# A planner's step table, landing time and ranks replaced, and one input load moved to ScalarE's queue, in a hybrid encoder layer

## The chip, the cores and the metric

The kernel runs on one core of a Trainium2 chip. The metric is the device time of one execution in microseconds (us). Five engines work beside each other: TensorE (PE, with its weight loads as PEld), VectorE (DVE), ScalarE (ACT), GpSimd (POOL) and SyncE (SP); SP issues most of the transfers.

## The reference

One encoder layer on two sequences of 512 tokens (prompt and sample), width 1024, all in float32:

```python
def rms_norm(x, g):
    xf = x.astype(jnp.float32)
    y = xf * lax.rsqrt(jnp.mean(xf * xf, axis=-1, keepdims=True) + EPS)
    return (y * g.astype(jnp.float32)).astype(x.dtype)

def swiglu(x, w_gate, w_up, w_down):
    return (jax.nn.silu(x @ w_gate) * (x @ w_up)) @ w_down
```

The layer is a half-weighted SwiGLU FFN (inner width 2816), a mixing block, a second such FFN and a final norm. The mixing block normalizes once and projects once; from that come grouped-query attention (8 query heads, 2 key heads of 64, rotary angles, softmax over 512 keys) and a bidirectional mLSTM memory (4 heads of 128, exponentials of gate sums as weights on q k^T, a row norm). Each is projected to the model width, both are gated per channel by a sigmoid and merged, and one output projection follows.

## The kernel before

Precision is kept by splitting: a float32 value becomes a high part (ScalarE copies it to fp32r) and a low part (VectorE subtracts the high part), and each product is three matmuls (high x high, high x low, low x high) of 512 columns. The FFNs and the gate projections use seven products of half blocks in place of eight, with sums of blocks of weights and inputs written by VectorE. So a weight costs a load on SP, a "high" on ScalarE (L247, L832, L2111) and a "low" on VectorE (L248, L835, L2114) before TensorE may use it, and a product costs an evacuation of its bank.

The first FFN fills 0 to about 640 us, the mixing block of both sequences about 640 to 1440, the second FFN the rest. The FFNs' order is written by hand. The order of the mixing block, with its seams to the FFNs, comes from a planner that runs while the kernel is built (`class Plan`, L719). Each piece of work is a task with an engine, a step (how long the engine is held), an end (when its result may be used), its dependencies, and the slots it needs and frees (banks, buffers). The planner keeps a clock per engine; at each step it takes, over all engines, the task that can start first, and among those of one engine that can start within 0.01 us the one with the lowest rank. The rank is

```python
t.rank = pri + self.n * 1e-3 + RANK.get(f"{self.part} {eng} {fn.__name__}", 0)
```

with a priority by kind (0 urgent, 2 and 3 weights, 5 for long rows of filling matmuls), the number of the task, and an entry of `RANK` (L702) for the part of the block, the engine and the function. The steps come from `ACT_STEP` and `DVE_STEP` (L789) by the width of the instruction; a helper's `more` adds to one, and `n` multiplies one for chains of small instructions. A transfer is given its bytes at 400 KB per us and `LANDING` (L791) us. None of this runs on the chip: the emitted order is pinned, each engine works through its own list in that order, and semaphores make it wait where an input is not there.

Names that the change and the steps below touch, with their lines before the change:

- `sums_stage` (L2163): scales the rows by their norm (L2167 on ScalarE, L2168 on VectorE), transposes them on TensorE (L1702), copies them out with the gain (L2197, tiles `t`), stores part of them to `xn1buf` (L2205), and builds sums and differences of blocks (L2217 on VectorE, high L2209 on ScalarE, low L2212 on VectorE, tiles `xc`). `seven` (matmuls at L2125) uses them for the gates, L2155 evacuates its banks `mm` to tiles `f`, and L2289 to L2302 make sums of weight blocks.
- `gates_rest` (L2268): the products that need these sums; L2316 takes their bank `pss`.
- kv, k, q and gates of the mixing block: L883 matmuls in token blocks, kv high and low at L816 and L819; the gate sums' matmuls L1055 need `Lt` (L1061).
- attention: scores L1225, after transposes of q at L1149 copied out at L1152.
- the memory heads, four for each sequence: 20 exponentials of 128 columns for each head (L1430, tiles `t` from `box` and `st`), q k^T products (L1441, bank `pss`), transposes of the weighted product (L1500), copied out (L1504) and split (L1508), output products with `Vm` (L1515, bank `pso`), squares of the output (L1526), their transposes (L1535). L853 are matmuls of the projections for the next head.
- the merge of the memory (`up_mem`): L1586 multiplies a gate onto the product in a bank `mm` and so frees the bank, L1589 adds it to `mg`, L816 and L819 make the high part `mh` and the low part `ml`; the output projection (L883, with `mh` and `ml`) follows. Beside it the next sequence's rows are transposed (L1702), copied out (L2090), stored to `xnbuf` (L2096) and split (L2097, L2098).
- `load_x` (L1708): loads chunks of the transposed input; L1761 and L1762 split them for the first products.

## Time and profile before

| | |
|---|---|
| time, median of 3 runs | 2045.89 us (2043.71 to 2048.75) |
| the profiled execution's own time | 2045.49 us |
| its span, first to last instruction | 2043.7 us |
| mean granted TensorE clock | 0.998 |
| TensorE busy, share of the span | 2024.0 us, 99% |
| TensorE weight loads busy | 1675.0 us, 82% |
| VectorE busy | 1593.8 us, 78% |
| ScalarE busy | 969.0 us, 47% |
| first matmul starts, last one ends | 1.04 us, 2033.3 us |

A row of the timeline reads: start in us from the span's start, length in us, engine, line of the kernel, operation, output and inputs by tile name, shapes, how many in a row, and in brackets how long the engine stood idle before it and what ended that. "SPq" and "ACTq" are the issues of transfers by SP and ScalarE. A row of waits reads: engine, operation's tile and line, the releaser, total us, times, longest. Lines are those of the kernel before; from L718 on the changed kernel has the same code one line further down.

### The profile page before, as it was taken

How to read it: one execution, taken by the hardware profiler on the slowest of the kernel's cores; microseconds unless marked ns; L12 is line 12 of the kernel's file. 1: busy time of each engine (PE TensorE's matmuls, PEld its weight loads, DVE VectorE, ACT ScalarE, POOL GpSimd, SP SyncE). 2: the span in 40 equal slices, each digit the busy share in tenths (PEclk: the TensorE clock that was granted, in tenths of full speed). 3: DMA queues.
4: the chain of work that ended last, by engine and by line, in shares of the span. 5: the costliest groups of instructions: out<-in, count | busy, mean ns of one | idle time of the engine just before them, and what ended most of it. 6: DMA issues, size and time to landing. Idle time of an engine off the chain costs nothing.

```text
span 2043.7 us, 26087 instructions
## 1 busy us (share of the span) xinstructions
PE 2024.0 (99%) x9340; PEld 1675.0 (82%) x9340; DVE 1593.8 (78%) x2532; ACT 969.0 (47%) x1620; POOL 24.5 (1%) x49
## 2 busy tenths in 40 slices
PE   9999999999999999999999999999999999999997
PEld 7888888888888788887888888888788888888886
DVE  7997888786796764896887866875888787776687
ACT  7543434342227533676644774655443444343224
POOL 0000000001000000000000000000000000000001
PEclk9999999999999999999999999999999999999999
DMA  9556555799774645312344322464464644389753
GB/s 340 185 169 223 182 189 202 245 367 354 249 253 148 218 141 181 107 45 83 124 132 163 130 83 73 149 220 148 133 236 164 218 166 153 134 296 398 271 199 143
DMA packets 149633, 389.02 MB, mean 190 GB/s; under 512 B 15232, under 2 KB 15296, under 8 KB 147712
## 3 DMA queue, kind: packets, MB, share of 16 engines
q1 hardware_dynamic: 148784, 385.60, 54.6%
q0 software_dynamic: 432, 1.25, 0.2%
q8 instruction: 73, 1.20, 0.2%
q10 hardware_dynamic: 288, 0.52, 0.1%
q14 instruction: 56, 0.46, 0.1%
HBM read 269.31 MB, written 118.00 MB: 190 GB/s over the span
## 4 chain that ended last, share of the span: by engine, by line
PE 89%; DVE 4%; ACT 3%; DMA 2%; issue 1%; SPq 0%; DVEq 0%; ACTq 0%
PE pss L292 17%; PE pst L292 11%; PE mm L853 10%; PE mm L292 8%; PE mm L553 7%; PE mm L883 7%; PE pst L553 4%; PE pss L553 4%; PE pss L2125 3%; PE pso L553 2%; PE pso L883 2%; PE pst L2125 2%; PE mm L2125 2%; PE pss L1225 1%; PE pst L1249 1%
## 5 line engine op out<-in xcount | busy, mean ns | idle before, releaser
L292 PE MATMUL pss<-xc,w 128*128 128x512 f32 x1632 | 389.7, 389 | 2.5 <-DVE t L322 0.9
L292 PEld LDWEIGHTS pss<-xc,w 128*128 128x128 f32 x1632 | 305.9, 188 | 68.2 <-DVE t L322 1.7
L247 ACT ACTIVATE w<-wr 128x1024 fp32r<-128x1024 f32 (+2 forms) x123 | 127.5, 1038 | 223.2 <-PE pst L292 118.0
L248 DVE TENSOR_TENSOR w<-wr,w 128x1024 fp32r<-128x1024 f32 (+2 forms) x123 | 147.0, 1197 | 60.2 <-ACT w L247 60.0
L292 PE MATMUL mm<-xc,w 128*128 128x512 f32 x792 | 190.4, 390 | 0.8 <-ACT xc L1761 0.6
L553 PE MATMUL mm<-w,rt 128*128 128x512 f32 x792 | 185.3, 389 | 0.0
L292 PEld LDWEIGHTS mm<-xc,w 128*128 128x128 f32 x792 | 148.3, 188 | 32.5 <-ACT xc L1761 1.3
L553 PEld LDWEIGHTS mm<-w,rt 128*128 128x128 f32 x792 | 148.5, 188 | 30.8
L292 PE MATMUL pst<-xc,w 128*128 128x512 f32 x528 | 127.0, 389 | 0.0
L292 PE MATMUL pst<-xc,f 128*128 128x512 f32 x528 | 126.8, 389 | 0.0
L835 DVE TENSOR_TENSOR w<-wr,w 128x1024 fp32r<-128x1024 f32 (+1 forms) x80 | 93.7, 1171 | 30.1 <-ACT w L832 29.3
L292 PEld LDWEIGHTS pst<-xc,w 128*128 128x128 f32 x528 | 99.1, 188 | 20.7
L292 PEld LDWEIGHTS pst<-xc,f 128*128 128x128 f32 x528 | 99.1, 188 | 20.6
L613 ACT ACTIVATE w<-t 128x512 fp32r<-128x512 f32 x82 | 51.6, 632 | 122.1 <-PE pst L553 63.6
L613 ACT ACTIVATE w<-wr 128x512 fp32r<-128x512 f32 x72 | 44.7, 631 | 128.2 <-PE pso L553 67.7
L832 ACT ACTIVATE w<-wr 128x1024 fp32r<-128x1024 f32 (+1 forms) x80 | 80.8, 1015 | 43.4 <-PE pso L883 26.8
L553 PE MATMUL pss<-w,rt 128*128 128x512 f32 x396 | 94.4, 389 | 0.5 <-ACT w L613 0.5
L553 PE MATMUL pst<-w,rt 128*128 128x512 f32 x396 | 94.0, 389 | 0.0
L553 PEld LDWEIGHTS pss<-w,rt 128*128 128x128 f32 x396 | 74.3, 188 | 16.2 <-ACT w L613 0.9
L553 PEld LDWEIGHTS pst<-w,rt 128*128 128x128 f32 x396 | 74.3, 188 | 15.4
L2125 PE MATMUL mm<-xc,w 128*128 128x512 f32 x360 | 83.9, 391 | 1.3 <-ACT f L2155 1.3
L2125 PEld LDWEIGHTS mm<-xc,w 128*128 128x128 f32 x360 | 67.1, 188 | 15.6 <-ACT f L2155 1.8
(404 smaller groups left out, 3896.3 us busy)
## 6 DMA issues: line engine op xcount, KB each, us to landing
rt<-rbuf SPq DMA_DIRECT2D x154, 512.0 KB, 5.7
rbuf<-t SPq DMA_DIRECT2D x72, 512.0 KB, 3.5
wr<-in_ffn_w_gate_dram SPq DMA_DIRECT2D x60, 512.0 KB, 4.3
wr<-in_w_in_cols_dram SPq DMA_DIRECT2D x48, 512.0 KB, 4.0
wr<-in_ffn_w_up_dram SPq DMA_DIRECT2D x44, 512.0 KB, 3.7
rbuf<-f SPq DMA_DIRECT2D x30, 512.0 KB, 4.0
rbuf<-tab SPq DMA_DIRECT2D x30, 512.0 KB, 3.9
wr<-in_ffn_w_down_dram SPq DMA_DIRECT2D x48, 256.0 KB, 6.3
```

The costliest lines, as they stand in the source:

```text
L247: pin(nc.scalar.activation(t[:, 0], src, AF.Copy))
L248: pin(V_.tensor_tensor(t[:, 1], src, f(t[:, 0]), op=ALU.subtract))
L292: pin(nc.tensor.matmul(p, a[:, k, :], xt[:, b, k, :], start=(first and k == 0 and i == 0), stop=(k == HK_ - 1 and i == 2), skip_group_chec ...
L553: nc.tensor.matmul(p, r[:, b, d * P:(d + 1) * P], u[:, a, :], start=(first and q == 0 and k == 0), stop=(q == len(us) - 1 and k == 2), ski ...
L613: nc.scalar.activation(hi, src, AF.Copy)
L832: own(nc.scalar.activation(c["hi"], c["raw"], AF.Copy))
L835: own(V_.tensor_tensor(c["lo"], c["raw"], f(c["hi"]), op=ALU.subtract))
L853: own(nc.tensor.matmul(b["p"], w_[:, k, cols], x_, start=(k == 0 and i == 0), stop=(k == n - 1 and i == 2)))
L883: own(nc.tensor.matmul(b[q][:, :N], x_[:, q * P:(q + 1) * P], w_[:, kl, :], start=(k == 0 and i == 0), stop=(k == KD - 1 and i == 2)))
L1225: own(nc.tensor.matmul(p, G["qT"][:, h, b * P:(b + 1) * P], G["kv"][:, h // 4 * 2 + j, :], start=(j == 0), stop=(j == 1)))
L1249: own(nc.tensor.transpose(p[:, b * P:(b + 1) * P], G["e", h, b // 2][:, b % 2, kb * P:(kb + 1) * P], ident))
L2125: own(nc.tensor.matmul(bank[name], left()[a][:, k, :], xcl[m][:, y, k, :], start=bool(first) and k == 0 and i == 0, stop=(k == HK_ - 1 and ...
```

## The change

Four things are replaced. `RANK` gets other keys and values (61 entries before, 65 now, few in common). The step tables and `LANDING` get other numbers, and so do eight `n` and `more` arguments. Where the planner's tasks are the same, their order is not: of the rows in which the emitted lists are compared (repeats folded), 3439 lines differ on TensorE, 2096 on ScalarE, 3124 on VectorE, 885 on SP, all between the first FFN's end and the second one's beginning but for one: the load of the second input chunk goes from SP, behind the first half weight and the gain, to ScalarE's queue, behind the first chunk and ahead of the table load. The numbers of instructions of each engine stay as they were, but for that transfer.

```diff
-    RANK = {"gsums ACT copy": 10.5, "k0 DVE k_scale": 10, "keys0 PE turn_k": 4, "rotate0 ACT high": -0.5,
...
-            "up_mem1 PE fn": -0.79, "up_mem1 DVE add": 7, "after1 PE turn": 1.17, "next ACT left_a": -5.5}
+    RANK = {"gsums ACT <lambda>": 5, "gsums ACT copy": 5, "grest ACT p_high": -7, "kv0 ACT raw": 0.09,
...
+            "sums ACT high": 2, "sums DVE low": 8}

-    ACT_STEP = {8: 0.2, 32: 0.2, 128: 0.3, 256: 0.33, 384: 0.45, 512: 0.51, 544: 0.7, 1024: 0.97}
-    DVE_STEP = {8: 0.11, 32: 0.12, 64: 0.14, 96: 0.28, 128: 0.26, 256: 0.34, 384: 0.48, 512: 0.61, 544: 0.65, 1024: 1.14}
-    SPARE, LANDING = 0.12, 1.9
+    ACT_STEP = {8: 0.12, 32: 0.15, 128: 0.18, 256: 0.33, 384: 0.48, 512: 0.59, 544: 0.6, 1024: 1.03}
+    DVE_STEP = {8: 0.11, 32: 0.12, 64: 0.14, 96: 0.28, 128: 0.26, 256: 0.34, 384: 0.5, 512: 0.67, 544: 0.7, 1024: 1.16}
+    SPARE, LANDING = 0.12, 2.3

-        root_q = dve(32, hold("rq", lambda: rstd_cols(G["ssq"], 32, DA, own)), reds, 0, n=18)
+        root_q = dve(32, hold("rq", lambda: rstd_cols(G["ssq"], 32, DA, own)), reds, 0, n=19.5)
-        t = act(32, gate_exp, [t], 0, more=2.8)
+        t = act(32, gate_exp, [t], 0, more=1.55)
...
-        scaled = dve(32, scales, [u], 1, (), ["pt"], n=20)
+        scaled = dve(32, scales, [u], 1, (), ["pt"], n=21.3)
...
     load_x(0, 0, 1, nc.scalar)
+    load_x(0, 1, 2, nc.scalar)
     load_half(0, 0)
     pin(nc.sync.dma_start(g1, I["ffn1_norm"]))
     warm = cpool.tile([P, 1], F32, name="warm")
     nc.scalar.activation(warm, ones[:, 0:1], AF.Silu)
-    load_x(0, 1, 2)
     load_x(0, 2, 3)
```

The lines left out are further entries of `RANK` and five more such arguments: the attention's `exp` (`more` 0.2 to 0.12), two `sq` (0.2 to 0.04) and two `left_sums` (`n` 5 to 4.25 and to 5.6).

**First place: ScalarE's list in the gate sums, about 670 to 685 us.** `w_` are weights made high, `f2_354` takes evacuated banks `mm_`, `xc_364` and `xc_367` are the first two block sums of the second half; `t2_356` is what one VectorE instruction writes only after the store from it has landed. Before:

```order
L2111 ACTIVATE w_386_5037<-wr_374_4907 128x1024
L2197 ACTIVATE t2_357_4830<-pst_377_4921,gain_2_93 128x512
L2197 ACTIVATE t2_357_4830<-pst_380_4939,gain_2_93 128x512
L2155 ACTIVATE f2_354_4827<-mm_385_5017 128x512
L2209 ACTIVATE xc_364_4864<-t2_357_4830 128x1024
L2209 ACTIVATE xc_367_4867<-t2_356_4829 128x1024
L2155 ACTIVATE f2_354_4827<-mm_383_4980 128x512
L2111 ACTIVATE w_388_5081<-wr_378_4927 128x1024
L2155 ACTIVATE f2_354_4827<-mm_387_5061 128x512
L2209 ACTIVATE xc_365_4865<-t2_316_4679 128x1024
```

and now:

```order
L2112 ACTIVATE w_386_5034<-wr_370_4889 128x1024
L2156 ACTIVATE f2_354_4827<-mm_385_5016 128x512
L2198 ACTIVATE t2_356_4829<-pss_377_4924,gain_2_93 128x512
L2198 ACTIVATE t2_357_4830<-pst_378_4931,gain_2_93 128x512
L2198 ACTIVATE t2_356_4829<-pss_379_4939,gain_2_93 128x512
L2198 ACTIVATE t2_357_4830<-pst_380_4947,gain_2_93 128x512
L2210 ACTIVATE xc_364_4864<-t2_357_4830 128x1024
L2156 ACTIVATE f2_354_4827<-mm_383_4979 128x512
L2112 ACTIVATE w_388_5078<-wr_372_4899 128x1024
L2156 ACTIVATE f2_354_4827<-mm_387_5055 128x512
L2210 ACTIVATE xc_367_4867<-t2_356_4829 128x1024
```

Before, `xc_367`, which waits for VectorE and the store, stands ahead of the evacuation of `mm_383` and all that follows; now the evacuations of `mm_383` and `mm_387` stand ahead of it, and the four copies with the gain stand behind the evacuation of `mm_385`.

**Second place: ScalarE's list in the first memory head of the first sequence, about 960 to 970 us.** `Vm_733` is the value tile's last high part, `t2_749` to `t2_763` take the exponentials, `pst_747` and `pst_748` hold the third and the fourth transposed block, `pso_` the head's output. Before:

```order
L816 ACTIVATE Vm_733_7326<-pso_740_7382 128x512
L1430 ACTIVATE t2_749_7513<-box_468_5958,st_513_6301 128x128
L1430 ACTIVATE t2_750_7516<-box_468_5958,st_513_6301 128x128
L1430 ACTIVATE t2_749_7513<-box_468_5958,st_513_6301 128x128 x4
L1430 ACTIVATE t2_750_7516<-box_468_5958,st_513_6301 128x128 x2
L1504 ACTIVATE t2_759_7547<-pst_747_7494 128x512
L1430 ACTIVATE t2_750_7516<-box_468_5958,st_513_6301 128x128 x2
L1504 ACTIVATE t2_761_7558<-pst_748_7507 128x512
L1430 ACTIVATE t2_762_7564<-box_468_5958,st_513_6301 128x128
L1430 ACTIVATE t2_763_7567<-box_468_5958,st_513_6301 128x128
L832 ACTIVATE w_764_7569<-wr_752_7524 128x1024
```

and now, from the third exponential on (the last copy of `Vm` and two exponentials stand ahead):

```order
L1431 ACTIVATE t2_750_7515<-box_468_5958,st_511_6292 128x128
L1431 ACTIVATE t2_751_7518<-box_468_5958,st_511_6292 128x128
L1431 ACTIVATE t2_749_7513<-box_468_5958,st_511_6292 128x128 x4
L1431 ACTIVATE t2_750_7515<-box_468_5958,st_511_6292 128x128 x4
L1431 ACTIVATE t2_751_7518<-box_468_5958,st_511_6292 128x128 x4
L1505 ACTIVATE t2_762_7563<-pst_747_7494 128x512
L1431 ACTIVATE t2_763_7568<-box_468_5958,st_511_6292 128x128 x3
L1505 ACTIVATE t2_765_7578<-pst_748_7507 128x512
L1431 ACTIVATE t2_763_7568<-box_468_5958,st_511_6292 128x128 x2
L833 ACTIVATE w_766_7587<-wr_754_7532 128x1024
L833 ACTIVATE w_767_7596<-wr_756_7538 128x1024
L1527 ACTIVATE t2_768_7599<-pso_757_7542 128x512
```

Before, 8 exponentials stand between the last copy of `Vm` and the copy of `pst_747`; now 15 stand there, 3 more ahead of the copy of `pst_748`, and two weights in a row ahead of the squares.

**Third place: VectorE's list at the end of the second sequence's merge, about 1352 to 1360 us.** `mm_1389` (before) and `mm_1380` (now) are the last banks of the merge, freed by the gate; `ml_` are low parts that wait for ScalarE's high parts. Before:

```order
L835 TENSOR_TENSOR w_1379_11213<-wr_1362_11111,w_1379_11213 128x1024
L819 TENSOR_TENSOR ml_1375_11181<-mg_1034_9329,mh_1374_11180 128x512 x2
L2098 TENSOR_TENSOR xc_1292_10726<-f2_1383_11230,xc_1292_10726 128x512
L1586 SCALAR_TENSOR_TENSOR t2_1340_10997<-t2_1340_10997,mm_1382_11223 128x512
L2098 TENSOR_TENSOR xc_1292_10726<-f2_1383_11230,xc_1292_10726 128x512
L2098 TENSOR_TENSOR xc_1292_10726<-f2_1387_11256,xc_1292_10726 128x512
L1589 TENSOR_TENSOR mg_1034_9329<-mg_1034_9329,t2_1338_10988 128x512
L2098 TENSOR_TENSOR xc_1292_10726<-f2_1387_11256,xc_1292_10726 128x512
L1589 TENSOR_TENSOR mg_1034_9329<-mg_1034_9329,t2_1338_10988 128x512
L1589 TENSOR_TENSOR mg_1034_9329<-mg_1034_9329,t2_1339_10992 128x512
L819 TENSOR_TENSOR ml_1375_11181<-mg_1034_9329,mh_1374_11180 128x512 x3
L1586 SCALAR_TENSOR_TENSOR t2_1340_10997<-t2_1340_10997,mm_1389_11272 128x512
```

and now:

```order
L820 TENSOR_TENSOR ml_1376_11200<-mg_1029_9313,mh_1375_11199 128x512 x3
L1587 SCALAR_TENSOR_TENSOR t2_1340_11003<-t2_1340_11003,mm_1374_11185 128x512
L1587 SCALAR_TENSOR_TENSOR t2_1341_11009<-t2_1341_11009,mm_1377_11207 128x512
L836 TENSOR_TENSOR w_1373_11181<-wr_1361_11124,w_1373_11181 128x1024
L1587 SCALAR_TENSOR_TENSOR t2_1341_11009<-t2_1341_11009,mm_1380_11230 128x512
L836 TENSOR_TENSOR w_1379_11222<-wr_1362_11129,w_1379_11222 128x1024
L836 TENSOR_TENSOR w_1382_11251<-wr_1364_11133,w_1382_11251 128x1024
L1590 TENSOR_TENSOR mg_1029_9313<-mg_1029_9313,t2_1339_11000 128x512
L1590 TENSOR_TENSOR mg_1029_9313<-mg_1029_9313,t2_1340_11003 128x512
L2099 TENSOR_TENSOR xc_1290_10718<-f2_1386_11267,xc_1290_10718 128x512
L820 TENSOR_TENSOR ml_1376_11200<-mg_1029_9313,mh_1375_11199 128x512
```

Before, the last gate stands behind three low parts `ml_1375`; now the last gate stands ahead of the additions and the splits of the transposed rows.

More of the change, by code (lines that the diff above doesn't have):

```diff
@@ L700, in encoder @@
     outs_of = []
[L702 removed]
[3 rows of a table removed]
[L706 to L712 removed]
[3 rows of a table removed]
[L716 to L717 removed]
+    RANK = {"gsums ACT <lambda>": 5, "gsums ACT copy": 5, "grest ACT p_high": -7, "kv0 ACT raw": 0.09,
+            "k0 DVE k_cos": 14.5, "q0 SP w_fetch": -7.19, "gates0 DVE <lambda>": 3, "keys0 PE turn_k": 51.5,
+            "rotate0 DVE low": -2, "mem_qk0 SP w_fetch": -2, "mem_qk0 DVE w_low": 15, "mem_qk0 ACT high": -24.5,
[4 rows of a table added]
+            "up_mem0 DVE add": 6, "after0 DVE low": 4.5, "kv1 ACT w_high": -1.5, "kv1 DVE w_low": 5.5,
+            "kv1 ACT raw": 0.5, "q1 ACT w_high": -1.5, "out1 ACT w_high": -1.5, "out1 DVE w_low": -14,
[6 rows of a table added]
+            "up_mem1 PE fn": -4.5, "up_mem1 DVE add": 7.5, "after1 ACT copy": -3, "sums ACT copy": 30.5,
+            "sums ACT high": 2, "sums DVE low": 8}
     class Plan:
@@ L1241, in mix @@
                 first = [exps[h - h % 2, 0]] if h % 2 or b else []
-                exps[h, b] = act(512, exp, [u, *first] + ([exps[h, b - 1]] if b % 2 else []), 1, ["prob"] if b % 2 == 0 else (), ["ps"], more=0.2)
+                exps[h, b] = act(512, exp, [u, *first] + ([exps[h, b - 1]] if b % 2 else []), 1, ["prob"] if b % 2 == 0 else (), ["ps"], more=0.12)
             bank = ("o", "mm")[h % 2]
@@ L1622, in done @@
                     u = dve(512, add, [t, into[h]], 1)
-                    ends.append(act(512, sq, [u], 1, (), [bank_of(q)], more=0.2))
+                    ends.append(act(512, sq, [u], 1, (), [bank_of(q)], more=0.04))
                     dma(lambda: nc.sync.dma_start(x2buf[1][:, h, q, :], x()), [u], 2, kb=256)
```

14 lines of the change are left out of this document (3 added, 11 removed), and 16 rows, old and new, of the table RANK.

## The prediction

> **What bounds the kernel now.** I read the page first: the span and the chain that ended last.
>
> ```profile
> span 2043.7 us, 26087 instructions
> ...
> PE 89%; DVE 4%; ACT 3%; DMA 2%; issue 1%; SPq 0%; DVEq 0%; ACTq 0%
> ```
>
> TensorE holds 89% of the last chain. Then the table by windows, for the stretch from 640 to 1440 us in which the planner writes the order; its columns are the length, the busy time of TensorE, of its weight loads, of VectorE, ScalarE and GpSimd (number of instructions), the granted clock, the DMA share and GB/s.
>
> ```profile
> 640.00:1440.00 800.00, 795.36 (x3918) 660.10 (x3917) 598.10 (x1131) 471.86 (x905) 2.70 (x20) 1.00 0.41 135
> ```
>
> TensorE is busy 795.36 of 800 us there, at full clock. The change adds no matmul and removes none, so it can only move the time in which TensorE waits: 4.6 us here, two stalls at the seam behind it (0.57 and 0.69, below) and one of 0.44 at the start. Two rows of TensorE's waits that no later part shows (total us, times, longest):
>
> ```profile
> PE pss L1702 <- ACT xs L2167: 0.4, 1, 0.4
> ...
> PE pst L1055 <- DVE Lt L1061: 0.2, 1, 0.2
> ```
>
> A stall costs a little more than the idle time that is recorded. In the timeline of TensorE (start, length, line, operation, count, idle time before it with its releaser):
>
> ```profile
> 962.16 0.96 PE L1515 MATMUL pso<-t,Vm 128*128 128x512 f32 x3 [0.28 <-DVE Vm L819]
> ...
> 967.39 0.61 PE L853 MATMUL mm<-xc,w 128*128 128x512 f32 x2
> 968.58 0.66 PE L1535 MATMUL pst<-ident,t 128*128 128x128 f32 x4 [0.58 <-ACT t L1526]
> ...
> 1399.10 8.10 PE L2125 MATMUL mm<-xc,w 128*128 128x512 f32 x35
> ...
> 1433.69 6.74 PE L2125 MATMUL mm<-xc,w 128*128 128x512 f32 x29
> ```
>
> 35 matmuls of the last two kinds take 8.10 us and 29 take 6.74, so one more takes 0.227. Two start at 967.39, the next was due at 967.84 and came at 968.58: 0.74 us late for 0.58 us recorded. With 0.16 us for each of some eleven stalls the planned part with its seam can give back 4.6 + 1.3 + 1.8 = 7.7 us and the start 0.6. **All of it is 8 us, 0.4% of the time**; on the other side there is no such floor.
>
> The sum is made against the profiled execution, 2045.49 us (2043.7 us of span and 1.8 us around it). The median of the runs shown is 2045.89, so 0.4 us is added at the end. A measurement of this kernel can tell about 0.3%, 6.1 us, from no change.
>
> **The start.** The second input chunk is issued by ScalarE behind the first instead of by SP behind the first weights and the gain.
>
> ```profile
> 1.63 1.38 SPq L1709 DMA_DIRECT2D xt<-in_x_prompt_t_dram  x3
> ```
>
> ```profile
> 0.72 0.41 ACTq L1709 DMA_DIRECT2D xt<-in_x_prompt_t_dram  x1
> ...
> 7.11 2.01 ACT L1761 ACTIVATE xc<-xt,g 128x512 fp32r<-128x512 f32 x3 [0.83 <-DMA xt<-in_x_prompt_t_dram]
> ```
>
> ```profile
> 7.88 0.50 PE L292 MATMUL mm<-xc,w 128*128 128x512 f32 x1 [0.44 <-ACT xc L1761]
> ```
>
> SP issued three chunks in 1.38 us, 0.46 us each; ScalarE's own first issue ends at 0.72 + 0.41 = 1.13, so the chunk leaves at about 1.14 instead of 1.63, and the two behind it on SP move up by 0.46. ScalarE waited 0.83 us for the second chunk and TensorE then 0.44 us. I take **-0.4 us**. Bounds: the whole stall, -0.6, and 0 if the landing is set by the traffic and not by the issue. What is queued behind the new issue on ScalarE is its table load and the warm-up activation; they slide by 0.4 us, and the time in which ScalarE waits for the first weights covers them. Without that cover the start would lose those 0.4 us again.
>
> **First transposes and the gate sums, 642 to 693 us.** In the new order the first transposes stand 13 matmuls (13 x 0.227 = 2.9 us) later, behind the scaling that they waited for, but the second half of that scaling also stands later on ScalarE, behind two weight copies. Of the 0.6 us (0.4 recorded + 0.16) I take **-0.3**, between -0.6 and +0.3.
>
> ScalarE, VectorE and TensorE from the timeline, and the store from the table of transfers (count, size, median us from issue to landing):
>
> ```profile
> 671.66 0.63 ACT L2155 ACTIVATE f<-mm 128x512 f32<-128x512 f32 x1
> 672.13 1.10 ACT L2209 ACTIVATE xc<-t 128x1024 fp32r<-128x1024 f32 x1
> 677.17 1.06 ACT L2209 ACTIVATE xc<-t 128x1024 fp32r<-128x1024 f32 x1 [3.94 <-DVE t L2217]
> 678.14 0.58 ACT L2155 ACTIVATE f<-mm 128x512 f32<-128x512 f32 x1
> ```
>
> ```profile
> 675.91 1.23 DVE L2217 TENSOR_TENSOR t<-t,t 128x1024 f32<-128x1024 f32 x1 [2.63 <-DMA xn1buf<-t]
> ...
> 692.30 1.23 DVE L2114 TENSOR_TENSOR w<-wr,w 128x1024 fp32r<-128x1024 f32 x1 [3.16 <-ACT w L2111]
> ...
> 698.75 3.49 DVE L2114 TENSOR_TENSOR w<-wr,w 128x1024 fp32r<-128x1024 f32 x3
> ```
>
> ```profile
> 678.77 14.58 PE L2125 MATMUL mm<-xc,w 128*128 128x512 f32 x63 [1.34 <-ACT f L2155]
> ...
> 700.03 3.03 PE L2125 MATMUL pss<-xc,w 128*128 128x512 f32 x12 [0.34 <-DVE w L2114]
> ```
>
> ```profile
> xn1buf<-t SPq DMA_DIRECT2D x2, 512.0 KB, 6.1
> ```
>
> The row at 678.77 is the longest stall. VectorE waits 2.63 us for a store to land, ScalarE's L2209 (677.17) waits for VectorE, and the evacuation L2155 that TensorE needs (678.14) stands behind L2209. In the new order (first place in the section on the change) that evacuation, a weight copy and another evacuation stand ahead of the L2210 that depends on the store. So 1.34 + 0.16 go: **-1.5** (bounds -1.5 and 0). The price is that the four copies that feed the stores now all stand behind the evacuation that ran at 671.66, so the stores leave near 674.5 (four copies of 0.6 us from 672.1); before, all four stood ahead of it. With the 6.1 us of the last row they land between 680 and 681, where VectorE went on at 675.91 before. It has one weight copy and one subtraction less to do behind that point (2 x 1.13 us, from the three in 3.49), and so ends its chain about 4.6 - 2.3 = 2.3 us later; it had 3.16 us of idle time ahead of 692.30, so I take **0**, up to +1.0 if both stores are slow. **Behind that**, the low half of the second weight of the gates stood behind six instructions on VectorE (it is the first of the three at 698.75) and now follows the first low half directly: **-0.5** for 0.34 + 0.16; 0 if another wait takes its place.
>
> [...]
>
> **Lt and the other small ones.** The tiny matmuls that wait for Lt (L1055) stand later than Lt's new place on VectorE needs: **-0.3**. The wait at L883 for the low half of kv stays, since the weight copy that holds VectorE up there still stands ahead. The first attention scores now stand four matmuls (0.9 us) behind the last transposes of q, and two copies of 0.6 us stand between: **+0.3**, bounds 0 and +0.5.
>
> **The first part of the memory heads, 940 to 1020 us.** Here I expect a loss.
>
> ```profile
> 961.28 2.44 ACT L1430 ACTIVATE t<-box,st 128x128 f32<-128x128 f32 x8
> 963.62 0.59 ACT L1504 ACTIVATE t<-pst 128x512 fp32r<-128x512 f32 x1
> ```
>
> ```profile
> L1430 ACT ACTIVATE t<-box,st 128x128 f32<-128x128 f32 x160 | 49.7, 393 | 0.1
> ```
>
> Eight exponentials took 2.34 us (961.28 to 963.62), 0.293 each from start to start; the 393 ns of the last row overlap. The planner had 0.30 us for a 128-wide ScalarE step and now has 0.18. The new order (second place) puts 15 of them, not 8, between the last copy of Vm and the copy L1505 that TensorE's third output product needs: 15 x 0.293 = 4.4 us, where the new table sees 2.7. On the clock of before: exponentials 961.28 to 965.7, copy 965.7 to 966.3; TensorE begins the first output product at 962.16 as before, when the low half of Vm is there, has 12 matmuls ahead of the third (2.7 us) and reaches it at 964.9: it waits 1.4 us. Three more exponentials and the next copy end at 967.6 (0.6 us more of waiting), then two exponentials and the weight copy at 969.2 (0.7 more), then another weight copy and L1527 at 970.6, which the squares wait for. The squares ran at 968.58 before, so this place loses 970.6 - 968.6 = **+2.0**. At the next two heads 13 exponentials stand ahead of L1527: 13 x (0.293 - 0.18) = 1.5 us more than the planner thinks, of which I take **+0.8** and **+0.5**, because memory projections stand beside them as cover. Bounds for the three: 0 (the projections cover all) and +6 (2.0 at each). For the heads of the second sequence I take nothing: there the exponentials stand ahead of waits that are late anyway.
>
> **Out projection, 1357 us.**
>
> ```profile
> 1357.60 0.73 PE L883 MATMUL mm<-w,mh 128*128 128x512 f32 x2 [0.94 <-DVE t L1586]
> ```
>
> ScalarE's copy L2090 waited for a store, three low parts L819 on VectorE waited for what stands behind it on ScalarE, and the gate L1586 that frees TensorE's bank stood behind them. In the new order (third place) all gates of that part stand ahead of the low parts and the transposes come after the last unit: **-1.1** (bounds -1.1 and 0).
>
> **The seam to the second FFN, 1440 to 1450 us.**
>
> ```profile
> 1441.45 2.58 PE L292 MATMUL pss<-xc,w 128*128 128x512 f32 x10 [0.57 <-DVE w L2114]
> ...
> 1448.12 2.14 PE L292 MATMUL pss<-xc,w 128*128 128x512 f32 x8 [0.69 <-DVE t L322]
> ```
>
> Two stalls: 0.57 us on the low half of a weight, and 0.69 on L322. The first goes, since that weight is written four instructions earlier on VectorE. For the second the answer is open: a subtraction on a late-loaded weight (L268, which followed L322 before) now stands ahead of the work that leads to L322, but TensorE also has ten more matmuls (2.3 us) ahead of its wait for L322. If that load takes the 6.1 us of the store above, the seam loses up to 1.2 us net; if it takes 4 us, it gains 1.1. I take **0**.
>
> **Sum:** -0.4 - 0.3 - 1.5 - 0.5 - 0.3 + 0.3 + 2.0 + 0.8 + 0.5 - 1.1 = -0.5. 2045.49 - 0.5 + 0.4 = **2045.4 us**: what the new order takes out at the two long stalls it gives back at the memory heads. With every bound on its good side the terms make -0.6 - 0.6 - 1.5 - 0.5 - 0.3 - 1.1 - 1.1 = -5.7, so 2040.2; with every one on its bad side 0.3 + 1.0 + 0.5 + 6 + 1.2 = +9.0, so 2054.9.
>
> **Rivals.** *The stalls go and nothing comes back*: projections stand beside the exponentials as cover. For it: between these heads TensorE has units of 24 matmuls, 5.4 us each. Against it: the waiting copy stands in ScalarE's own queue behind the exponentials, so cover on TensorE must stand ahead of the waiting matmul, and at the first head there is none. -4.1 in all: 2041.8; with the seam's gain 2040.7.
>
> *Slower, through the step of 0.18 us*: my reading of the five other heads is too kind, and each pays what the first does. It decides where 11 or more exponentials stand between the last thing released and a copy that TensorE waits for (11 x 0.113 = 1.2 us of error, more than the 0.9 us of four matmuls). With 2.0 us at each of 7 further heads instead of 1.3 for two: +12.7, so 2058.1; with half of that 2051.8. For it: 160 exponentials x 0.113 = 18 us that the new planner does not see. Against it: ScalarE is busy 472 of the 800 us, so most copies find it idle.
>
> *The change doesn't do what it says*: TensorE is never short of ready matmuls for long, so another order moves nothing that can be seen: 2045.9.
>
> **How the numbers follow.** Forecast (2042.5 to 2049.5) 0.45; nothing moves 0.15, inside the same band; stalls gone 0.17; slower through the exponentials 0.23. Faster by over 0.3% (below 2039.8) needs the second rival and more than I can find: 0.12. Slower by over 0.3% (above 2052) is most of the third and some of the forecast's bad side: 0.25. Within 0.3%: 0.63. The range takes in the good bounds and half of the slower rival: 2040 to 2053.
>
> **What would show it.** Right: no TensorE wait on the evacuation of line 2156 near 678 us, none on L1587 near 1357, and new waits of some 1.4 us on the output product L1516 and of 0.5 to 1 on L1536 near 962 to 971, with 15 exponentials in a row on ScalarE just before them, 0.293 us apart. Wrong: if these exponentials stand under running matmuls (then the second rival), or if waits on L1516 and L1536 come at all eight heads, or if a store that takes over 7 us stalls the gates at 693.

## The result, and the profile after

The changed kernel takes 2050.88 us (median; 2047.64 to 2054.59), the kernel before 2045.64 us in the same series (2043.71 to 2049.22). The ratio is 1.0022, with a 95% interval of 1.0016 to 1.0029: **4.5 us slower** by the ratio, which is not the quotient of the two medians (they differ by 5.2 us). The forecast was 2045.4 us; the time lies inside its range of 2040 to 2053, and inside the 0.3% that it called "same", but outside the likeliest case (2042.5 to 2049.5), and the forecast had the time fall a little where it rose. The profiled execution took 2049.88 us, 4.4 more than the one of before.

The page of the changed kernel, its span and the shares of the last chain by engine:

```profile
span 2048.0 us, 26069 instructions
...
PE 85%; DVE 3%; ACT 2%; DMA 2%; issue 1%; SPq 0%; DVEq 0%; ACTq 0%
```

The bound is the same, TensorE; its busy time is 2024.9 us against 2024.0. So the 4.3 us of span are time in which it waits or runs slowly, and the table by windows says in which stretch. Of before (columns as in the prediction; the second number is TensorE's busy time):

```profile
640.00:800.00 160.00, 157.77 (x711) 128.49 (x710) 107.65 (x141) 74.98 (x110) 0.00 (x0) 1.00 0.51 172
900.00:1100.00 200.00, 199.13 (x1015) 166.12 (x1014) 156.65 (x349) 123.41 (x258) 1.36 (x10) 1.00 0.33 107
...
1440.00:1500.00 60.00, 58.74 (x258) 47.93 (x258) 47.92 (x62) 22.77 (x31) 0.00 (x0) 1.00 0.54 176
```

and of after:

```profile
640.00:800.00 160.00, 159.97 (x725) 131.41 (x724) 109.20 (x142) 76.73 (x112) 0.00 (x0) 1.00 0.52 178
900.00:1100.00 200.00, 195.72 (x989) 161.95 (x988) 151.47 (x343) 121.72 (x254) 1.35 (x10) 1.00 0.32 103
...
1440.00:1500.00 60.00, 56.70 (x242) 46.12 (x241) 47.68 (x61) 22.93 (x31) 0.00 (x0) 0.97 0.48 157
```

In the first row TensorE is now hardly ever idle: 2.2 us won. In the second, the memory heads, it idles 4.3 us in place of 0.9. In the last, the seam to the second FFN, it idles 3.3 in place of 1.3, and the granted clock is 0.97, where before has 1.00. TensorE's waits of after name both places (total us, times, longest):

```profile
PE pst L292 <- ACT t L326: 3.2, 1, 3.2
PE pst L1536 <- ACT t L1527: 2.9, 4, 0.9
```

**The seam.** TensorE's timeline of after around it:

```profile
1446.71 1.52 PE L292 MATMUL mm<-xc,w 128*128 128x512 f32 x6
1451.47 3.35 PE L292 MATMUL pst<-xc,w 128*128 128x512 f32 x7 [3.24 <-ACT t L326]
```

ScalarE's timeline of after there:

```profile
1449.88 1.06 ACT L247 ACTIVATE w<-wr 128x1024 fp32r<-128x1024 f32 x1 [6.26 <-DVE wr L271]
1450.84 0.58 ACT L326 ACTIVATE t<-pst 128x512 f32<-128x512 f32 x1
```

and VectorE's:

```profile
1446.47 0.69 DVE L270 TENSOR_TENSOR wr<-tab,wr 128x512 f32<-128x512 f32 x1
1448.55 0.69 DVE L268 TENSOR_TENSOR t<-wr 128x512 f32<-128x512 f32 x1 [1.39 <-DMA wr<-in_ffn_w_up_dram]
1449.16 0.68 DVE L271 TENSOR_TENSOR wr<-wr 128x512 f32<-128x512 f32 x1
```

Read upward from TensorE: it wants the bank `pst` again, which L326 evacuates. L326 takes half a microsecond and TensorE had gone on from that bank by 1446.7, but on ScalarE it stands behind the weight copy L247, L247 needs VectorE's L271, and L271 stands behind L268, the first of four sums of halves (one addition, three subtractions) for the *next* pair of weights, whose load lands at 1448.5. In the kernel before, L268 stood behind L271, L248 and L322. VectorE's timeline of before:

```profile
1443.70 0.69 DVE L270 TENSOR_TENSOR wr<-tab,wr 128x512 f32<-128x512 f32 x1
1444.43 0.69 DVE L271 TENSOR_TENSOR wr<-wr 128x512 f32<-128x512 f32 x1
1446.25 1.23 DVE L248 TENSOR_TENSOR w<-wr,w 128x1024 fp32r<-128x1024 f32 x1 [1.13 <-ACT w L247]
1447.39 0.68 DVE L322 TENSOR_TENSOR t<-t,pss 128x512 f32<-128x512 f32 x1
1448.61 0.69 DVE L268 TENSOR_TENSOR t<-wr 128x512 f32<-128x512 f32 x1 [0.54 <-DMA wr<-in_ffn_w_up_dram]
```

Two more things differ. VectorE comes to L270 2.8 us later than before (1446.47 against 1443.70), and TensorE's second product into `pst` stands ahead of the one into `pss`, where before it stood behind it. And the seven matmuls behind the wait take 3.35 us, twice their usual time; the windows there show why (the granted clock is the third number from the end):

```profile
1451.40:1454.00 2.60, 2.53 (x6) 2.05 (x7) 2.60 (x4) 0.54 (x2) 0.00 (x0) 0.50 0.21 60
1454.00:1457.00 3.00, 3.00 (x13) 2.39 (x13) 0.10 (x1) 0.00 (x0) 0.00 (x0) 0.87 0.31 123
```

0.50 for 2.6 us and 0.87 for 3 us make 2.6 + 3 x 0.13/0.50 = 3.4 us at half the clock, which costs 1.7 us in this execution.

**The first memory head.** ScalarE's timeline of after:

```profile
958.00 0.60 ACT L817 ACTIVATE Vm<-pso 128x512 fp32r<-128x512 f32 x1 [1.23 <-PE pso L884]
958.49 4.48 ACT L1431 ACTIVATE t<-box,st 128x128 f32<-128x128 f32 x15
962.88 0.58 ACT L1505 ACTIVATE t<-pst 128x512 fp32r<-128x512 f32 x1
...
967.20 0.58 ACT L1527 ACTIVATE t<-pso 128x512 f32<-128x512 f32 x1
```

VectorE's, one row:

```profile
960.67 0.69 DVE L1451 SCALAR_TENSOR_TENSOR t<-pss,t 128x512 f32<-128x512 f32 x1 [1.15 <-ACT t L1431]
```

and TensorE's:

```profile
961.42 0.96 PE L1442 MATMUL pss<-qk 128*128 128x512 f32 x3 [0.95 <-DVE t L1451]
...
966.40 0.73 PE L854 MATMUL mm<-xc,w 128*128 128x512 f32 x2 [0.31 <-ACT w L833]
967.83 0.65 PE L1536 MATMUL pst<-ident,t 128*128 128x128 f32 x4 [0.70 <-ACT t L1527]
```

The 15 exponentials take 962.88 - 958.49 = 4.39 us, 0.293 each, as forecast, where the planner counts 0.18. TensorE feels them first at the q k^T product L1442, which wants a bank that VectorE's L1451 frees, and L1451 waits for exponentials (0.95 us); then at the weight of L854 (0.31) and at the squares (0.70).

For the experiments one number for each stretch is needed that clock and waits both enter: **lost time**, the time from start to start of successive matmuls beyond the step that their kind takes when nothing waits (0.2267 us for 512 columns, 0.124 for 272, 0.109 for 128), summed over the stretch from the trace. Before has 23.4 us of it, after 27.7: the 4.3 us of span. By stretch, with four of the runs told below; the stretches left out, 100 to 600 us and behind 1600, make the rest of the last column:

| lost time, us | 0-100 | 600-800 | 800-900 | heads 900-1100 | 1100-1400 | seam 1400-1600 | all |
|---|---|---|---|---|---|---|---|
| before | 5.5 | 5.0 | 2.0 | 3.4 | 4.0 | 1.9 | 23.4 |
| after | 5.0 | 1.6 | 2.3 | 8.2 | 3.6 | 5.5 | 27.7 |
| before, thin exponentials | 5.4 | 5.2 | 2.0 | 2.7 | 5.3 | 1.8 | 23.6 |
| after, thin exponentials | 4.9 | 2.3 | 2.3 | 3.7 | 3.6 | 5.7 | 25.0 |
| after, seam pinned | 4.8 | 1.5 | 2.3 | 8.2 | 3.0 | 3.8 | 25.5 |
| after, both | 4.9 | 1.7 | 2.3 | 3.8 | 2.5 | 3.5 | 20.3 |

One trace is one execution. Some waits on transfers come and go between traces of the same order: one near 1130 us in the order of before costs nothing in its own trace and 1.0 to 1.6 us in three others. Such a row moves a total by 1 to 2 us, so the stretches are compared here, and the totals by the ratios.

### The profile page after: what moved, and what is told of

The parts are those of the page before. It is cut to its first block, busy times and chain, and to the rows that moved or that the text cites. A ratio compares the mean times of both kernels' runs of the same rounds, so it can differ in the third digit from the quotient of the medians.

```text
span 2048.0 us, 26069 instructions
## 1 busy us (share of the span) xinstructions
PE 2024.9 (99%) x9340; PEld 1675.9 (82%) x9340; DVE 1596.1 (78%) x2532; ACT 969.0 (47%) x1620; POOL 26.3 (1%) x49
## 4 chain that ended last, share of the span: by engine, by line
PE 85%; DVE 3%; ACT 2%; DMA 2%; issue 1%; SPq 0%; DVEq 0%; ACTq 0%
PE pss L292 15%; PE mm L854 10%; PE pst L292 10%; PE mm L553 8%; PE mm L884 7%; PE mm L292 6%; PE pst L553 4%; PE pss L553 4%; PE pss L2126 3%; PE mm L2126 3%; PE pso L553 3%; PE pso L884 2%; PE pst L2126 2%; PE pst L1250 1%; PE pss L1226 1%; ACT t L1431 1%
## 5 line engine op out<-in xcount | busy, mean ns | idle before, releaser
L247 ACT ACTIVATE w<-wr 128x1024 fp32r<-128x1024 f32 (+2 forms) x123 | 127.3, 1038 | 223.5 <-PE pst L292 128.3
L248 DVE TENSOR_TENSOR w<-wr,w 128x1024 fp32r<-128x1024 f32 (+2 forms) x123 | 146.9, 1196 | 57.9 <-ACT w L247 57.6
```

What stands on the lines that cost most here:

```text
L247: pin(nc.scalar.activation(t[:, 0], src, AF.Copy))
L248: pin(V_.tensor_tensor(t[:, 1], src, f(t[:, 0]), op=ALU.subtract))
```

## The experiments

Two theories stood against each other. **A**: the loss sits at the seam. **B**: it sits at the memory heads, through exponentials dearer than the new table says, and the seam's wait would come back elsewhere. A third, **C**, came in with the second kind of test: ranks are worth something only with the table that they were searched with.

Each ratio is to executions of the kernel before in the same series; their medians are 2046.91 us for e1_seam to e4_step, 2046.33 for e5_bthin to e8_seam_step and 2046.43 for e9_local and e10_gates. A difference of two such ratios is uncertain by about 0.001, 2 us.

**e1_seam: the seam alone.** In the second FFN the four sums of the second pair of weights are pinned in program order, so L268 no longer jumps the queue.

```diff
-more = gu_left_b(*raw, ring, left, *([tc.keep_in_program_order] if i == 1 and ahead else []))
+more = gu_left_b(*raw, ring, left, *([tc.keep_in_program_order] if i == 1 and (ahead or at is None) else []))
```

> The changed kernel, but at the seam to the second FFN the four sums of weight halves (L268 to L271) of the second pair of weights are pinned in program order, so that L268 on a load that lands late no longer stands ahead of L271 of the weight before it. The order ahead of 1440 us is that of the changed kernel. Theory A (the loss sits at the seam: VectorE waits 1.39 us for that load, L271 and then ScalarE's weight copy L247 wait behind it, the evacuation L326 waits behind L247, and TensorE idles 3.24 us and then runs at a granted clock of 0.50 for some 2.6 us): L271 can run at 1447.2, L247 at 1447.8, L326 at 1448.8, so TensorE waits 1.2 to 1.8 us instead of 3.24, and the clock stays at 1.00; 2.5 to 3.5 us come back, about 2047.7 us, ratio to the kernel before 1.0008 (1.0004 to 1.0012). Theory B (the memory heads carry the loss and the seam's wait would come back somewhere later): no more than 1 us comes back, ratio 1.0017 to 1.0022. Also told apart: if the clock falls to 0.50 behind a wait under 2 us as well, it is not the length of the wait that sets it.

Measured: 2048.87 us, ratio to before 1.0005 (0.9997 to 1.0014). TensorE at the seam, from the timeline of this run:

```profile
1449.21 1.68 PE L292 MATMUL pst<-xc,w 128*128 128x512 f32 x6 [1.76 <-ACT t L326]
```

ScalarE there:

```profile
1447.62 1.06 ACT L247 ACTIVATE w<-wr 128x1024 fp32r<-128x1024 f32 x1 [4.32 <-DVE wr L271]
1448.58 0.58 ACT L326 ACTIVATE t<-pst 128x512 f32<-128x512 f32 x1
```

and the window with its clock:

```profile
1448.00:1451.00 3.00, 1.79 (x8) 1.43 (x9) 2.30 (x3) 1.68 (x3) 0.00 (x0) 1.00 0.23 74
```

The wait is 1.76 in place of 3.24 us, and the matmuls behind it run at full clock (six in 1.68 us). By the ratios 0.0017, 3.5 us, came back; by the two traces 2.2. The place itself gives back 2.9 us (5.0 to 2.0 of lost time), but two waits that neither before nor after has come in at 1514.4 and 1520.4 us (0.50 on L322 and 0.23 on L331, 1.3 us of lost time), behind a pin that changes VectorE's list up to there. So some of it does come back elsewhere, as B says, though not most. The heads' rows are unchanged (8.2 us in the table), and B is not out for the rest. And 1.76 us of the wait stay: VectorE is still 2.5 us later at L270 than before (1446.16), and `pst` still stands ahead of `pss` on TensorE. Which of these two it is, no run separates.

**e2_thin and e5_bthin: the exponentials, with and without the change.** Eight columns in place of 128, everything else in its place.

```diff
-    G["W", h, i] = wide("t2")
+    G["W", h, i] = wide("t2"); own(nc.gpsimd.memset(G["W", h, i].rearrange("p d (b c) -> p d b c", c=P)[:, :, :, 8:], 1.0))
...
-own(nc.scalar.activation(G["W", h, i][:, d, b * P:(b + 1) * P], src, AF.Exp, bias=bias))
+own(nc.scalar.activation(G["W", h, i][:, d, b * P:b * P + 8], src[:, 0:8], AF.Exp, bias=bias))
```

> The changed kernel with the same order on TensorE, VectorE and ScalarE, but each of the 160 exponentials of the memory heads does 8 columns in place of 128; the other 120 are set to 1 by GpSimd beforehand, which is otherwise idle. The output so leaves out these exponentials. It makes an exponential cost about 0.2 us in place of 0.293, near the 0.18 that the planner took, without another order. Theory B (exponentials dearer than planned are what holds up the copies that TensorE waits for): the waits at 934.7, 961.4, 964.9, 966.4, 967.8, 983.8, 1012.3 and 1305.8 us, 6.4 us of loss together, fall to 2 or less: 4 to 5 us come back, about 2046.4 us, ratio 1.0004 (0.9998 to 1.0008). Theory A (the seam is the loss; the waits at the heads are there in both kernels and only moved): 0.5 to 1.5 us come back, ratio 1.0016. The seam's 3.24 us stay in both.

> The kernel before with the same thinning as in the run that thinned the changed kernel: 8 columns for each of the 160 exponentials of the memory heads, the rest set to 1 by GpSimd (these exponentials are left out of the output), with the order of before on TensorE, VectorE and ScalarE. It gives the other corner of the comparison. If the order of the change is what made the price of the exponentials felt, thin exponentials are worth little here: the trace of before has 0.45 + 0.74 us of loss at the first head and nothing at the next ones, so 0 to 1.2 us, ratio 0.9997 (0.9994 to 1.0001). If thin exponentials take as much out of the kernel before as out of the changed one (some 6 us by the ratios, 1.0022 to 0.9990), then the heads are no part of the change's loss, and the ratio is 0.997 to 0.998.

Measured: the changed kernel comes to 2045.24 us, ratio 0.9990 (0.9981 to 0.9999); the kernel before to 2044.59 us, ratio 0.9994 (0.9985 to 1.0003). ScalarE of the thinned changed kernel at the first head, from the timeline:

```profile
959.38 2.96 ACT L1431 ACTIVATE t<-box,st 128x8 f32<-128x8 f32 x15
962.25 0.58 ACT L1505 ACTIVATE t<-pst 128x512 fp32r<-128x512 f32 x1
```

and TensorE:

```profile
961.60 0.96 PE L1442 MATMUL pss<-qk 128*128 128x512 f32 x3 [0.24 <-DVE t L1451]
```

15 thin ones take 962.25 - 959.38 = 2.87 us, 0.19 each, and the wait of 0.95 us falls to 0.24. The heads' stretch falls from 8.2 to 3.7 us of lost time in the changed kernel, from 3.4 to 2.7 in the kernel before. So the price of the exponentials is felt 4.5 us there with the new order and 0.7 with the old one: 3.8 us of the difference at the heads are theirs. By the ratios they are worth 0.0032 (6.5 us) and 0.0006 (1.2 us); by the totals of the traces, in which other waits came in, 2.7 and nothing. Theory A's 0.5 to 1.5 us is out, and so is the reading that the heads are no part of the loss.

**e6_seam_thin: both taken out.** The two edits above together.

> The changed kernel with both causes taken out: the four sums at the seam pinned in program order, and the memory heads' exponentials thinned to 8 columns with the same order (these exponentials are left out of the output). If the two add up, the ratio is 1.0022 - 0.0017 - 0.0032 = 0.9973, some 2041.5 us on the clock of the kernel before, and the trace shows neither the wait of 3.24 us nor waits over 0.9 us at the heads: then the gains of the new order are real and two places gave them back. If they do not add up (one hides in the other, or the time is given back behind them) the ratio is 0.9985 or more.

Measured: 2043.07 us, ratio 0.9983 (0.9974 to 0.9991). The sum of the single effects, 0.9973, lies just outside the interval, but each of the two is itself uncertain by 0.0009. In the table they add: seam 3.5 as with the seam alone, heads 3.8 as with thin exponentials alone. The total of 20.3 us is 7.4 under after and 3.1 under before. But thin exponentials take something out of the old order too, so the fair partner is before with thin ones: 0.9994 against 0.9983, 2.2 us, which these intervals don't tell from nothing, and 23.6 against 20.3 in the traces, of which 1.4 is the wait near 1130 us that comes and goes. That the gains of the new order are real shows in the stretch from 600 to 800 us (5.2 against 1.7), not in the total; and the two places gave back more than that, 3.6 us at the seam and 4.8 at the heads against 3.4 won there.

**e4_step: the exponentials' price alone put right.**

```diff
 t = act(128, one, [m_t, scaled, exps[HA - 1, 3]] + ([] if first else [es[0][0]]), 1,
-        ["prob"] if first else ())
+        ["prob"] if first else (), more=0.11)
```

> The changed kernel with one number of its planner altered: the exponentials of the memory heads are planned at 0.29 us (their measured 0.293) in place of 0.18. The ranks stay, so from 930 us on the planner finds another order, and the seam keeps its bad one. Theory B (the step of 0.18 is the cause): the planner again puts matmuls ahead of the waits, the 6.4 us of waits at the heads fall to 3 or less, ratio 1.0004 to 1.0010. Theory C (ranks that were searched for one table are worth nothing with another, whichever is truer): new waits elsewhere take the place of those, ratio 1.0018 or more, up to 1.005.

Measured: 2049.81 us, ratio 1.0013 (1.0004 to 1.0022), between the two expectations and, by its interval, not told from either. TensorE's waits:

```profile
PE pst L292 <- ACT t L326: 3.2, 1, 3.2
PE mm L884 <- DVE t L1587: 1.4, 1, 1.4
PE pst L1536 <- ACT t L1527: 1.4, 1, 1.4
```

The rows on L1536 fall from 2.9 to 1.4 us, but a new wait of 1.4 on L1587 (at 1060.7 us) and smaller ones in the memory's projections come in; the heads' stretch loses 8.7 us. A true price for these exponentials does not bring back a good order by itself: theory C has its part.

**e8_seam_step: the seam pinned and all 128-wide steps back at 0.3.**

```diff
-ACT_STEP = {8: 0.12, 32: 0.15, 128: 0.18, 256: 0.33, 384: 0.48, 512: 0.59, 544: 0.6, 1024: 1.03}
+ACT_STEP = {8: 0.12, 32: 0.15, 128: 0.3, 256: 0.33, 384: 0.48, 512: 0.59, 544: 0.6, 1024: 1.03}
```

> The changed kernel with the four sums at the seam pinned in program order and one number of the step tables back: 128-wide steps of ScalarE at 0.3 us in place of 0.18; ranks, landing time and the other steps are the changed kernel's. A correct candidate for beating both. If a truer price is all that the planner needs: heads lose 2 us or less, the seam 1.8, ratio 0.9990 to 1.0000. If ranks searched for another table spoil it, as in the run that planned the memory heads' exponentials alone at 0.29: new waits, ratio 1.0005 or more.

Measured: 2047.23 us, ratio 1.0008 (0.9999 to 1.0017). TensorE's waits:

```profile
PE mm L884 <- DVE w L836: 0.8, 1, 0.8
PE pso L1265 <- DVE t L1259: 0.8, 1, 0.8
```

No wait on L1536 is left among the long ones, but others have come in ahead of it, in the attention at 924 to 938 us (L1265, L1226, L884), and the heads' stretch loses 8.5 us. Again C.

**e7_tables: the new tables with the old ranks.** The changed kernel with the `RANK` of before.

```diff
-RANK = {"gsums ACT <lambda>": 5, "gsums ACT copy": 5, "grest ACT p_high": -7, "kv0 ACT raw": 0.09,
...
+RANK = {"gsums ACT copy": 10.5, "k0 DVE k_scale": 10, "keys0 PE turn_k": 4, "rotate0 ACT high": -0.5,
...
```

> The changed kernel with the ranks of the kernel before: new step tables, new landing time, the input load on ScalarE, old RANK. The order is a third one, and at the seam L271 stands ahead of L268 again. If the tables are the cause (128-wide steps of 0.18 on ScalarE), the heads lose what they lose in the changed kernel while the seam does not: ratio 1.0005 to 1.0015. If ranks count only with the table that they were searched for, new waits of 5 us or more come in anywhere in 640 to 1440 us: ratio 1.0025 to 1.006.

Measured, in four executions: 2064.69 us, ratio 1.0094 (1.0078 to 1.0109), far over either expectation. TensorE's waits:

```profile
PE pst L1535 <- ACT t L1526: 4.3, 6, 1.4
PE mm L853 <- ACT mem L816: 1.5, 1, 1.5
PE pst L1055 <- DVE Lt L1061: 1.1, 1, 1.1
```

Tables and load without their ranks cost 19 us, and the new ranks win 15 of them back. Of the 40.9 us of lost time 13.2 lie at the heads and 11.3 at 1100 to 1400 us. So the change is not "better numbers plus a better order": the table alone makes the plan worse, and the search repaired most of that.

**e3_start: the load on ScalarE alone**, in the kernel before.

```diff
 load_x(0, 0, 1, nc.scalar)
+load_x(0, 1, 2, nc.scalar)
...
-load_x(0, 1, 2)
```

> The kernel before, with one part of the change alone: the second input chunk issued by ScalarE behind the first. Everything else is as before. By the prediction's step for the start 0.4 us less, ratio 0.9998; the bounds were 0 and -0.6, so 0.9997 to 1.0000. The traces of before and after differ by 0.47 us in the first 100 us. A ratio over 1.0005 or under 0.9993 would say that the issue does something later in the kernel that the two traces do not show.

Measured: 2046.03 us, ratio 0.9995 (0.9986 to 1.0004). The time can't tell 0.5 us from nothing; in the trace the first 100 us lose 5.0 in place of 5.5 us, and it is 4.8 to 5.0 in the traces of all ten kernels with that load on ScalarE, and 5.4 to 5.5 in the two without.

**e9_local and e10_gates: only what was worth something.** The old tables and ranks, the load on ScalarE, and three ranks of the change for the gate sums; e9_local also moves the gate L1586 of the second merge ahead of the low parts.

```diff
-RANK = {"gsums ACT copy": 10.5, "k0 DVE k_scale": 10, "keys0 PE turn_k": 4, "rotate0 ACT high": -0.5,
...
-        "up_mem1 PE fn": -0.79, "up_mem1 DVE add": 7, "after1 PE turn": 1.17, "next ACT left_a": -5.5}
+RANK = {"k0 DVE k_scale": 10, "keys0 PE turn_k": 4, "rotate0 ACT high": -0.5, "mem_qk0 DVE w_low": 41.5,
...
+        "up_mem1 PE fn": -0.79, "up_mem1 DVE add": 7, "after1 PE turn": 1.17, "next ACT left_a": -5.5,
+        "gsums ACT <lambda>": 5, "gsums ACT copy": 5, "grest ACT p_high": -7, "up_mem1 DVE gate": -5}
```

> The kernel before with its own tables and ranks, and from the change only what its traces showed to be worth something: the second input chunk on ScalarE's queue, the three ranks of the change for the gate sums (L2269 and L2273: two at 5, one at -7), and one new rank, the gate at L1586 of the second memory merge at -5, which puts it ahead of the three low parts L819. The order of before stays everywhere else: 11 matmuls of L2125, four instructions of ScalarE, one weight copy of VectorE and two gates move. Theory (the gains are local and need no new table): 0.5 at the start, 1.3 to 1.6 for the wait on L2155 at 678 us, 0 to 0.5 for the one at 700, 1.1 at 1357, in all 2.9 to 3.7 us, 2042.5 us, ratio 0.9984 (0.9980 to 0.9988); heads and seam as in the kernel before. Rival (such waits come back behind the place where they were taken out, as in the runs with other steps): ratio 0.9993 or more.

> The same without the rank for the gate at L1586: the kernel before with the input chunk on ScalarE's queue and the change's three ranks for the gate sums. Theory: 1.8 to 2.6 us less than before, ratio 0.9990 (0.9987 to 0.9992), and the wait of some 1.1 us at 1357 is there. Rival: if its ratio is that of the run with the gate's rank, the wait at 1357 was hidden anyway.

Measured: e9_local 2043.09 us, ratio **0.9985 (0.9976 to 0.9994)**; e10_gates 2043.74 us, ratio 0.9987 (0.9978 to 0.9995). Both are faster than the kernel before, and than the changed one; the interval of e9_local just reaches the rival's 0.9993. TensorE from 640 to 800 us in e9_local:

```profile
640.00:800.00 160.00, 159.47 (x721) 130.50 (x720) 108.55 (x141) 75.61 (x109) 0.00 (x0) 1.00 0.52 177
```

1.7 of the 2.2 us that the new order won there come with three ranks (e10_gates has 159.47 us there too), and heads (3.4) and seam (2.0) stay as they were before. The wait at 1357 us is gone in e9_local and there in e10_gates (0.87 us); the difference of their medians, 0.65 us, is too small to be told from none, so that last rank is shown by the trace and not by the time.

## Why the prediction was wrong

The mechanisms that it named for the planned part came for the most part as told; **the step that failed is the last one, the seam, taken at 0 with bounds of -1.1 and +1.2; it measured +3.6**, most of the miss. In the table "measured" is the lost time of after less that of before.

| step | forecast | measured |
|---|---|---|
| start | -0.4 | -0.5 |
| transposes, L2155, weight low, 640 to 800 us | -0.3 - 1.5 - 0.5 = -2.3 | -3.4 |
| stores late at 693 us | 0, up to +1.0 | no wait there |
| Lt and first scores | 0.0 | +0.3 |
| memory heads, first sequence | +3.3 | +4.8 |
| out projection | -1.1 | -1.1 |
| seam | 0 | +3.6 |
| all other places | 0 | +0.5 |

- **Seam.** The step said of VectorE's L268 on the late load: it "now stands ahead of the work that leads to L322, but TensorE also has ten more matmuls (2.3 us) ahead of its wait for L322". It followed only one road from L268, to L322 and the bank `pss`. The other road is L271, ScalarE's L247 and, behind L247 in ScalarE's own queue, L326, which frees `pst`; TensorE wanted `pst` after six matmuls. The "ten more matmuls" were no cover: 13 stand ahead of the wait for L322 where 3 stood, but seven of these go into `pst` and wait for L326 themselves. (L268 is an addition, not a subtraction; that changes nothing.) The load took 4.9 us from issue to landing (1443.6 to 1448.5), inside the 4 to 6.1 that the step weighed. The wait of 3.24 us and the half clock behind it (1.7 us) make the seam three times as dear as the upper bound. e1_seam shows that L268 ahead of L271 cost 1.5 us of the wait and, in this execution, the half clock; the cause of the 1.76 us that stay is open.
- **Heads.** The price and the size were right: 0.293 us an exponential, 15 of them ahead of the copy, the waits at 961 to 968 us (2.96 us of loss against 1.19 before: +1.8 for 2.0 forecast), then 0.85 for 0.8 and 1.07 for 0.5. The road was partly another: the 1.4 us forecast on the output product L1516 are 0.13 there, since TensorE had already lost 0.95 at L1442, through VectorE's L1451. What the sum left out is the same price at places that it had not read: a wait of 0.60 us at 934.7 behind seven exponentials, and one of 0.61 at 1305.8 in the second sequence, for which it took nothing.
- **640 to 800 us** gained 1.1 more than forecast: the wait at 650 us went altogether, and the one at 700 too. The 0 for the stores held, but not for its reason: they were to leave near 674.5 us and left at about 671, because the evacuation ahead of them ran at 668.49 and not at 671.66, and VectorE went on at 676.41 and not at 680 to 681. So its bound of +1.0 was never tried.
- **Start.** The stall on the second chunk went, with 0.2 us behind it, but the first weight came later (ScalarE's L247 at 5.11 against 4.74 us) and the first product began 0.38 us later, for which the step had no term. That -0.5 comes out so near to -0.4 is partly luck.
- **The rival "slower, through the step of 0.18 us"** had the right sign and, by e2_thin and e5_bthin, the right mechanism for 3.8 us at the heads, but it was priced at 6 to 13 us because it put 2.0 at every head; only the first one pays that. It had no term for the seam, and so it is one half of the answer.

What stays open: e8_seam_step shows that a truer step and a pinned seam are not enough, but not which order a search over ranks with 0.29 us would find; that wasn't tried.

## What to carry to other kernels

When an instruction that waits for a late transfer is moved up, follow every queue behind it to every bank that TensorE reuses, and not only the first consumer: here L268's wait of 1.39 us on VectorE travelled through L271 and ScalarE's L247 and L326 to TensorE, which waited 3.24 us with it and 1.76 without (e1_seam). A planner's table and the ranks searched with it are one thing; change one number and the order is a new draw, so the pieces of a new order that a trace shows to be good are better carried over one by one. And a wait on TensorE can cost more than its length: behind 3.24 us in the changed kernel and 3.09 in e2_thin the granted clock fell to 0.50 for 3.41 us, and in e7_tables behind a stretch of 3.41 us with 1.78 us of idle time in several pieces; behind 3.23 us in e4_step it did not.

## What the runs showed of the hardware

Behind gaps of nearly the same length, about 3 us, the clock fell in two runs and stayed up in a third. The same seven matmuls behind the same wait, first in e2_thin (TensorE's timeline):

```profile
1448.66 2.64 PE L292 MATMUL pst<-xc,w 128*128 128x512 f32 x7 [3.09 <-ACT t L326]
```

with the clock of the two windows that follow:

```profile
1448.60:1451.20 2.60, 2.54 (x8) 2.00 (x9) 2.60 (x4) 0.54 (x2) 0.00 (x0) 0.69 0.19 46
1451.20:1454.20 3.00, 3.00 (x11) 2.39 (x10) 0.10 (x1) 0.00 (x0) 0.00 (x0) 0.70 0.33 135
```

Then in e4_step:

```profile
1452.81 1.89 PE L292 MATMUL pst<-xc,w 128*128 128x512 f32 x7 [3.23 <-ACT t L326]
```

with the window that follows:

```profile
1452.80:1455.40 2.60, 2.60 (x11) 2.17 (x12) 2.60 (x4) 0.47 (x1) 0.00 (x0) 1.00 0.26 63
```

3.24 us idle in the changed kernel: half clock at once. 3.09 in e2_thin: some time at full clock, then half, in all (0.31 x 2.6 + 0.30 x 3.0)/0.50 = 3.4 us. 3.23 in e4_step: full clock throughout. 1.76 in e1_seam: full clock. So the gap's length alone does not tell the executions with a fall from the one without.

The clock records of the twelve traces have three falls between first and last matmul, each 3.41 us long: 1451.36 to 1454.77 in the changed kernel, 1449.56 to 1452.97 in e2_thin, 974.34 to 977.75 in e7_tables. In the 3.41 us ahead of them TensorE was busy for 0.28, 0.90 and 1.63 us. The last of these has no wait over 0.93 us (the 3.41 us ahead of the fall, then the fall):

```profile
970.92:974.33 3.41, 1.63 (x9) 0.97 (x8) 3.07 (x12) 3.02 (x6) 0.00 (x0) 1.00 0.44 111
974.34:977.75 3.41, 3.41 (x10) 2.64 (x9) 3.41 (x10) 1.43 (x3) 0.00 (x0) 0.50 0.40 148
```

In the traces of before and after every change of the clock lies a whole number of steps of 3.413 us behind the first record (5.19 and 4.11 us into the span): 595 in before, for the fall at 2036.12 us, behind the last matmul; 424, 425 and 597 in after, for 1451.36, 1454.77 and 2041.87. Counted in such steps from its own first record, the wait of 3.23 us in e4_step lies across two, of which TensorE was busy for 1.48 and 2.10 us, and the clock stays up. By the steps of the matmuls, as in the table of lost time, 3.3, 2.6 and 2.3 us of matmuls are missing in the 3.41 us ahead of the three falls, and in no other such step at full clock in the twelve traces more than 2.1. What makes the clock fall was not shown. Whether an execution of the changed kernel pays the 1.7 us at the seam may depend on where the wait lies among such steps: an estimate of the author's, from these three falls and e4_step.

An exponential of 8 columns with its bias from a tile takes 0.19 us from start to start (e2_thin), one of 128 columns 0.293 (after): a sixteenth of the columns for two thirds of the price. So a table by width is best read from rows of just that form.
